# Second norm's modulation on VectorE, the exponentials' table loaded in the output projection, and zero products ahead of routing matmuls

## The chip, the cores and the metric

One core of a Trainium2 chip runs the whole program. The metric is the device time of one execution in microseconds (us). PE is TensorE (matmuls), DVE VectorE, ACT ScalarE, POOL GpSimd, SP SyncE; ACT, POOL and SP also issue DMAs.

## The reference

Two layers of a diffusion backbone over 256 latent tokens and 256 context tokens, each row 1024 wide, all in float32. Each layer first mixes tokens (three attention-like mixers, gated, then an output projection) and then runs a mixture of 16 experts with top-2 routing. What bears on the change, from `hybrid_layer` and `moe_ffn`, cut:

```python
ctx = ctx + mc[2] * mix[:, :L]
x = x + m[2][:, None] * mix[:, L:]
hc = modulate(rms_norm(ctx, norm2), mc[3], mc[4])          # h * (1 + scale) + shift
hx = modulate(rms_norm(x, norm2), m[3][:, None], m[4][:, None])
...
probs = jax.nn.softmax((h @ w_router).astype(jnp.float32), axis=-1)
sel = (probs + b_router.astype(jnp.float32)).reshape(N, N_GROUPS, EXPERTS_PER_GROUP)
...
return (jax.nn.silu(xblk @ w_gate[e]) * (xblk @ w_up[e])) @ w_down[e]
```

Layer 0 does this for context and latent rows (512 rows, four tiles of 128), layer 1 for the latent rows alone (two tiles).

## The kernel before

The program is recorded through a layer that reorders instructions on each engine by their dependences, from the order of the code and from priorities; `issue_after` ties the start of a block to an instruction. All weights come from HBM through SP's queue into a few slots ahead of their use. For float32 precision a weight block is split by ACT into a rounded part `whi` (line 231) and by DVE into the rest `wlo` (line 232), and PE makes three products of each (lines 243 to 245).

The output projection (`output_projection`, lines 900 to 945) splits the merged mixers' output into `mh` and `ml`, then runs through two column halves `dh`; each has two weight pieces and every piece two pairs of `whi` and `wlo`. At the end of a tile and half, `done` adds the gated result to `x` (lines 921 and 922). `vectors` issues small loads from ACT's queue behind the last `mh` cast, in layer 0 also the broadcast rows `m34` (shift and scale of the second norm, line 840) and the norm's weight; a DVE product (line 1080) turns `m34[:, r, 1]` into (1 + scale) times the norm's weight.

`tile_done` (from line 1083) follows each tile of the second half: transposes, sum of squares, `rstd_of`, the router's eight matmuls (line 1099). In layer 0 ACT scales the row, POOL multiplies and adds the modulation in two halves (lines 1104 and 1105), and SP writes the row to `h2d` in HBM. In layer 1 ACT makes `hh` and DVE `hl` (line 1110), for the last tile POOL does so in two operations (lines 1113 and 1114). After each second tile `route` (line 1211) runs a long chain of small DVE operations from `mx` (line 1218) and the exponentials (line 1220) through `se` (line 1225) to `ohb`, the one-hot experts of the pair (line 1257). PE counts ranks from `ohb` (lines 1263 and 1264, the rank matmuls). In layer 0 `place_tiles` then builds one-hot matrices `M` (line 1299) and multiplies (line 1303) to place rows into experts' slots; `indices` makes `gix` (line 1324), by which POOL's indirect DMA gathers the rows of an expert from `h2d` (line 1361). The first expert begins with transposes of `xg` (line 1388). In layer 1 `place_group` gathers by products with `Mg` (line 1342). A branch for overflowing experts stands behind the routing.

`keep_warm` (line 136) multiplies zeros (`idle`, 128x32, against 512 columns) and is called at the program's start only. ACT keeps one table of functions at a time; the exponentials need a load ahead of them (ACT_TABLE_LOAD).

Of the kernel before, what the change touches and what calls it, by code (L numbers as in the profile page):

```python
# [12 lines left out]
F32 = mybir.dt.float32  # L13
# [5 lines left out]
AF = mybir.ActivationFunctionType  # L19
ALU = mybir.AluOpType  # L20
AX = mybir.AxisListType
# [46 lines left out]
def mk(ap, off, dims):  # L68
    return bass.AP(tensor=ap.tensor, offset=ap.offset + off, ap=[list(ap.ap[0])] + [list(d) for d in dims])
# [7 lines left out]
def kernel(es, tc, A, out, dbg=None):  # L77
    nc = tc.nc
    V, S, G, PE, SY = nc.vector, nc.scalar, nc.gpsimd, nc.tensor, nc.sync
# [7 lines left out]
    sm = es.enter_context(tc.tile_pool(name="sm", bufs=2))  # L87
# [3 lines left out]
    RAW_BUFS = 3  # L91
    ARAW = 1
    WARM0, WARM1 = 14, 4
    ORDER = "x0 x1 x2 x3 a0 w0 a1 a2 a3 w1 a4 a5 a6 a7"
    pb = {}

# [23 lines left out]
    rows = cst.tile([128, 512], F32, name="mr")[0:64, 0:128]  # L120
# [9 lines left out]
    nhalf = cst.tile([128, 8], F32, name="nhalf")  # L130
    V.memset(nhalf, -0.5)

    idle = cst.tile([128, 32], BF16, name="idle")
    V.memset(idle, 0.0)

    def keep_warm(n, tag="d"):
        ps = bank(tag)
        for _ in range(n):
            PE.matmul(ps[0:32], idle, mk(idle, 0, [[0, 16], [1, 32]]), start=True, stop=True)

    keep_warm(WARM0, "t")

# [760 lines left out]
    def output_projection(l, op, mg, x, vectors, loaded, tile_done):  # L903

        full = l == 0
        nt = 4 if full else 2
        mh = op.tile([128, 8, 128 * nt], F32R, name="mh")
        m2 = op.tile([128, 2 if full else 1, D], F32, name="m2")
        bcast_rows(m2, l, 2, 3)
        ml = op.tile([128, 8, 128 * nt], F32R, name="ml")  # L910
        for k in range(8):
            m = mg[k // 4][:, k % 4]
            last = S.copy(mh[:, k], m)
            V.tensor_tensor(ml[:, k], m, mh.bitcast(F32)[:, k], ALU.subtract)

        vectors(last)

        def done(t, dh, ps):
            cs = slice(512 * dh, 512 * dh + 512)
            tm = op.tile([128, 512], F32, name="tm", bufs=2)  # L920
            V.tensor_tensor(tm, ps, m2[:, 1 if full and t < 2 else 0, cs], ALU.mult)
            (V if dh else G).tensor_tensor(x[:, t, cs], x[:, t, cs], tm, ALU.add)

        raws = [raw_piece([A["w_out"][l, 512 * h:512 * h + 512, 512 * dh:512 * dh + 512]])
                for dh in range(2) for h in range(2)]
        for dh in range(2):
            w = []
            ps = {}
            for h in range(2):
                w.append(split_raw(*raws[2 * dh + h]))  # L930
                if dh == 1 and h == 1:
                    loaded()
                for t in range(nt) if dh == 0 or h == 1 else ():
                    for hh in (h,) if dh == 0 else (0, 1):
                        if hh == 0:
                            ps[t] = ps_g() if dh or t < 3 else ps_a()
                        for k in range(4):
                            sl = slice(128 * t, 128 * t + 128)
                            mm3(ps[t], mh[:, 4 * hh + k, sl], ml[:, 4 * hh + k, sl],
                                w[hh][0][:, k], w[hh][1][:, k], hh == 0 and k == 0, hh == 1 and k == 3)  # L940
                    if h == 1:

                        with tc.high_priority() if dh and t == nt - 1 else nullcontext():
                            done(t, dh, ps[t])
                            if dh and t:
                                tile_done(t - 1)
                            if dh and t == nt - 1:
                                tile_done(t)
# [33 lines left out]
    h2d = [tc.dram_tile([512, D], F32, name="h2d0")]  # L982
# [3 lines left out]
    def tail(l, mp, mgp, mg, side, other):  # L986


        full = l == 0
        nt = 4 if full else 2  # L990
        cap = 128 if full else 64
# [3 lines left out]
        x = xp.__enter__().tile([128, nt, D], F32, name="x")  # L995
# [9 lines left out]
        with ExitStack() as ms, ExitStack() as ps_:  # L1005
# [26 lines left out]
            with ExitStack() as rs_:  # L1032
# [13 lines left out]
                wrm = rp.tile([128, len(rr), 8, 16], F32, name="wrm")  # L1046
                blg = rp.tile([128, len(rr), 16], F32, name="blg")

                lgs, placed = [None], None

                def vectors(last):
                    with tc.issue_after(last.ins):
# [31 lines left out]
                def tile_done(t):  # L1084
                    r = 1 if full and t < 2 else 0
                    ss = sm.tile([128, 1], F32, name="ss")
                    hT = rp.tile([128, 8, 128], F32, name="h2T", bufs=2)
                    for g in range(2):
                        pt = ps_t((128, 4, 128))
                        for k in range(4):  # L1090
                            PE.transpose(pt[:, k], x[:, t, 128 * (4 * g + k):128 * (4 * g + k + 1)], ident)
                        (V.tensor_copy if g else S.copy)(hT[:, 4 * g:4 * g + 4], pt)
                    xn = xg[(t + 1) % 2] if full else rp.tile([128, D], F32, name="sq", tag="h2T", bufs=2)
                    S.activation(xn, x[:, t], AF.Square, accum_out=ss)
                    rs = rsx[:, t:t + 1]
                    rstd_of(rs, ss, D)
                    lg = bank("g", (128, 16))
                    for k in range(8):
                        PE.matmul(lg, hT[:, k], wrm[:, r, k], start=k == 0, stop=k == 7)
                    if full:  # L1100
                        S.activation(xn, x[:, t], AF.Copy, scale=rs)
                        for g in range(2):
                            cs = slice(512 * g, 512 * g + 512)
                            G.tensor_tensor(xn[:, cs], xn[:, cs], m34[:, r, 1, cs], ALU.mult)
                            G.tensor_tensor(xn[:, cs], xn[:, cs], m34[:, r, 0, cs], ALU.add)
                        SY.dma_start(h2d[l][128 * t:128 * (t + 1)], xn)
                    else:
                        S.activation(hh[:, t], x[:, t], AF.Copy, scale=rs)
                        if t < nt - 1:
                            V.scalar_tensor_tensor(hl_[:, t], x[:, t], rs, hh.bitcast(F32)[:, t],  # L1110
                                                   ALU.mult, ALU.subtract)
                        else:
                            G.tensor_scalar(xn, x[:, t], rs, None, ALU.mult)
                            G.tensor_tensor(hl_[:, t], xn, hh.bitcast(F32)[:, t], ALU.subtract)
                    if t % 2 == 0:
                        lgs[0] = rp.tile([128, 2, 16], F32, name="lg", bufs=2)
                    V.scalar_tensor_tensor(lgs[0][:, t % 2], lg, rs, blg[:, r], ALU.mult, ALU.add)
                    if t % 2 == 0:
                        return
                    later = route(rp, lgs[0], t, nt, br, wts, comb, ohb, rnk, rnb if full else None, rhs, utr, one, cnt)  # L1120
                    if full:
                        nonlocal placed
                        placed = place_tiles(rp, (t - 1, t), cap, iot, rnb, rhs, cc, None if t < nt - 1 else
                                    lambda g: indices(rp, cc, gix, six, g))
                    later()

                with tc.tile_pool(name=f"wo{l}", bufs=1, side=other) as op:
# [80 lines left out]
        slot_queue()  # L1208
        return xp, x, rest

    def route(rp, lg, t1, NT_, br, wts, comb, ohb, rnk, rnb, rhs, utr, one, cnt):

        t0 = t1 - 1
        T = lambda nm, *w: rp.tile([128, 2] + list(w), F32, name=nm, bufs=2)
        pr, se, a1, o1, o2, e = T("pr", 16), T("se", 16), T("a1", 16), T("o1", 16), T("o2", 16), T("e", 16)
        mx, sm_, v, w = T("mx"), T("sme"), T("v"), T("w", 3)
        bc = lambda x, n, k=1: mk(x, 0, [[k, 2], [0, n]])
        V.tensor_reduce(mx, lg, AX.X, ALU.max, negate=True)
        for i in range(2):
            S.activation(pr[:, i], lg[:, i], AF.Exp, bias=mx[:, i:i + 1], accum_out=sm_[:, i:i + 1])  # L1220
        if t1 == NT_ - 1:
# [37 lines left out]
        last = t1 == NT_ - 1  # L1259
# [29 lines left out]

        return weights  # L1290

    def place_tiles(mo, ts, cap, iot, rnb, rhs, cc, then):

        Ms = []
        for g in range(2):
            ps = ps_a((128, 8, 3))
            for i, t in enumerate(ts):
                M = mo.tile([128, cap, 8], BF16, name="M", bufs=2)
                V.tensor_tensor(M, iot[:, :, 8 * g:8 * g + 8], mk(rnb, 16 * t + 8 * g, [[0, cap], [1, 8]]), ALU.is_equal)
                Ms.append(M)  # L1300
            for e in range(8):
                for i, t in enumerate(ts):
                    PE.matmul(ps[:, e], Ms[-len(ts) + i][:, :, e], mk(rhs, 48 * t + 8 * g + e, [[16, 3]]),
                              start=i == 0, stop=i == len(ts) - 1)
            pc = ps.rearrange("p e c -> p c e")
            dst = cc[:, :, 8 * g:8 * g + 8]
            if ts[0] == 0:
                V.tensor_copy(dst, pc)
            else:
                V.tensor_tensor(dst, dst, pc, ALU.add)  # L1310
            if then:
                r = then(g)
        return r if then else None
# [386 lines left out]
```

## Time and profile before

| | |
|---|---|
| median of 3 runs | 1782.86 us (1781.37 to 1783.88) |
| time of the profiled execution | 1782.55 us |
| its span in the trace | 1780.5 us |
| mean granted clock of TensorE | 0.975 |
| busy: PE, DVE, ACT, POOL | 93%, 59%, 46%, 19% of the span |
| HBM | 370.48 MB read, 17.72 MB written |

The span is what the trace covers; the time lies 2.05 us above it. A granted clock of 1.0 is 2.4 GHz and 0.50 is 1.2 GHz. A timeline row has the start in us, the duration in us, engine, line, operation with output and inputs, and behind `[` how long the engine was idle ahead of it and which instruction ended that.

### The profile page before, as it was taken

The page shows a single profiled execution, that of the slowest core. Times are in us where ns is not written, and L with a number is a line of the kernel's source. Part 1 is how long each engine was busy: PE and PEld are TensorE (multiplying, and loading weights), DVE is VectorE, ACT ScalarE, POOL GpSimd, SP SyncE. Part 2 cuts the span into 40 slices and gives each one's busy share as a digit, 9 for nine tenths or more (in the row PEclk, how much of TensorE's full clock was granted, in tenths as well). Part 3 has the DMA queues.
Part 4 walks back from the last instruction along what each step waited for, and adds up shares of the span by engine and source line. Part 5 has one row for each costly group of instructions (what it writes and reads, how often), then busy time and mean ns, then how long its engine had stood idle before and what let it go on. Part 6 is the DMA issues. An engine that isn't in the chain of part 4 may idle for free. (4 is left out here: it accounts for less than half of the span.)

```text
span 1780.5 us, 24184 instructions
## 1 busy us (share of the span) xinstructions
PE 1663.4 (93%) x8912; PEld 1218.9 (68%) x8913; DVE 1047.0 (59%) x1907; ACT 816.7 (46%) x1353; POOL 345.9 (19%) x343
## 2 busy tenths in 40 slices
PE   8999999999999999599999987999999999799997
PEld 4657677887677888477877765878887887433332
DVE  4328473447876345788888888588548865401101
ACT  3313332336676432378877874434456773201100
POOL 0003130222210134301321113133313202100000
PEclk8999999999999999699999997999999999899999
DMA  9895747523212454599999951422435348899996
GB/s 292 285 306 188 253 156 262 175 83 84 59 49 48 105 204 166 185 344 366 367 330 370 356 186 67 125 84 86 142 94 139 89 99 325 301 387 387 387 353 255
DMA packets 263551, 380.01 MB, mean 213 GB/s; under 512 B 33014, under 2 KB 129782, under 8 KB 257920
## 3 DMA queue, kind: packets, MB, share of 16 engines
q1 hardware_dynamic: 251920, 361.19, 60.2%
q10 hardware_dynamic: 7184, 9.42, 1.7%
q0 software_dynamic: 4320, 7.75, 1.3%
q8 instruction: 74, 1.21, 0.3%
q14 instruction: 53, 0.43, 0.1%
HBM read 370.48 MB, written 17.72 MB: 218 GB/s over the span
## 5 line engine op out<-in xcount | busy, mean ns | idle before, releaser
L232 DVE TENSOR_TENSOR wlo<-wraw,whi 128x1024 fp32r<-128x1024 f32 (+2 forms) x368 | 438.7, 1212 | 179.2 <-ACT whi L231 168.4
L231 ACT CAST whi<-wraw 128x1024 fp32r<-128x1024 f32 (+2 forms) x368 | 369.6, 1023 | 174.9 <-PE psg L245 75.8
L243 PE MATMUL psg<-hTh,whi 128*128 128x512 f32 (+1 forms) x576 | 206.2, 360 | 0.0
L244 PE MATMUL psg<-hTl,whi 128*128 128x512 f32 (+1 forms) x576 | 204.9, 356 | 0.0
L245 PE MATMUL psg<-hTh,wlo 128*128 128x512 f32 (+1 forms) x576 | 204.1, 356 | 0.0
L243 PE MATMUL psg<-whi,hTh 128*128 128x512 f32 (+1 forms) x392 | 148.8, 384 | 2.2 <-ACT hTh L373 2.1
L244 PE MATMUL psg<-wlo,hTh 128*128 128x512 f32 (+1 forms) x392 | 148.3, 379 | 0.0
L245 PE MATMUL psg<-whi,hTl 128*128 128x512 f32 (+1 forms) x392 | 147.6, 380 | 0.5 <-DVE hTl L404 0.4
L243 PEld LDWEIGHTS psg<-hTh,whi 128*128 128x128 f32 x576 | 108.9, 189 | 26.2 <-issue 11.0
L245 PEld LDWEIGHTS psg<-hTh,wlo 128*128 128x128 f32 x576 | 108.9, 189 | 18.8 <-issue 6.1
L1464 PE MATMUL psg<-wraw,xT 128*64 128x512 f32 x512 | 120.5, 595 | 1.1 <-ACTq L1139 0.9
L244 PEld LDWEIGHTS psg<-hTl,whi 128*128 128x128 f32 x576 | 109.2, 190 | 16.1 <-issue 4.0
L243 PE MATMUL psg<-whi,xh 128*128 128x512 f32 x256 | 101.7, 397 | 0.7 <-ACT xh L1389 0.7
L244 PE MATMUL psg<-wlo,xh 128*128 128x512 f32 x256 | 99.9, 390 | 0.0
L245 PE MATMUL psg<-whi,xl 128*128 128x512 f32 x256 | 99.6, 390 | 0.0
L243 PEld LDWEIGHTS psg<-whi,hTh 128*128 128x128 f32 x392 | 74.4, 190 | 19.4 <-ACT hTh L373 3.8
L1464 PEld LDWEIGHTS psg<-wraw,xT 128*64 128x64 f32 x512 | 37.2, 137 | 72.7 <-issue 69.1
L245 PEld LDWEIGHTS psg<-whi,hTl 128*128 128x128 f32 x392 | 74.2, 190 | 16.9 <-DVE hTl L404 1.7
L244 PEld LDWEIGHTS psg<-wlo,hTh 128*128 128x128 f32 x392 | 74.5, 190 | 13.2 <-issue 0.5
L1468 ACT ACTIVATE act<-psg 128x256 f32<-128x256 f32 x16 | 6.1, 384 | 150.7 <-PE psg L1464 129.0
L587 ACT ACTIVATE P<-P,smx 128x512 f32<-128x512 f32 (+1 forms) x96 | 62.2, 648 | 22.2 <-DVE smx L586 19.7
L836 POOL TENSOR_TENSOR mg<-mg,gates 128x512 f32<-128x512 f32 (+1 forms) x32 | 38.1, 1199 | 172.2 <-DVE gates L835 126.3
(413 smaller groups left out, 3285.3 us busy)
## 6 DMA issues: line engine op xcount, KB each, us to landing
wraw<-in_w_down_dram SPq DMA_DIRECT2D x64, 1024.0 KB
wraw<-in_w_ada_dram SPq DMA_DIRECT2D x40, 1024.0 KB
wraw<-in_w_in_dram SPq DMA_DIRECT2D x144, 256.0 KB
wraw<-in_w_up_dram SPq DMA_DIRECT2D x32, 1024.0 KB
wraw<-in_w_gate_dram SPq DMA_DIRECT2D x32, 1024.0 KB
wraw<-in_w_gate_dram SPq DMA_DIRECT2D x64, 512.0 KB
wraw<-in_w_up_dram SPq DMA_DIRECT2D x64, 512.0 KB
wraw<-in_w_in_dram SPq DMA_DIRECT2D x24, 1024.0 KB
```

The source lines that it names most:

```text
L231: S.copy(hi[:, :, 0:n], r[:, 2 * j:2 * j + 2, 0:n])
L232: V.tensor_tensor(lo[:, :, 0:n], r[:, 2 * j:2 * j + 2, 0:n], hi.bitcast(F32)[:, :, 0:n], ALU.subtract)
L243: PE.matmul(ps, ah, bh, start=start, stop=False)
L244: PE.matmul(ps, ah, bl, start=False, stop=False)
L245: PE.matmul(ps, al, bh, start=False, stop=stop)
L587: S.activation(flat, flat, AF.Exp, scale=-1.0, bias=m[:, 0:1], accum_out=m[:, 2:3])
L836: G.tensor_tensor(dst, dst, sg[:, i], ALU.add)
L1464: PE.matmul(pgu[64 * c:64 * c + 64, :], xT[:, 2 * p + k, o:o + 64], r[:, :, k, 256 * c:256 * c + 256], start=p == 0 and k == 0, stop=p == ...
L1468: S.activation(a, pgu[:, 0:256], AF.Silu)
```

## The change

Four edits. `tile_done` in layer 0 computes the modulated row by two DVE operations over the whole row of 1024 (a scaled product with `m34[:, r, 1]`, then the addition) instead of ACT's copy and four POOL operations; in layer 1 the last tile's `hl` comes from the same DVE operation as the others'. For the last tile of either layer these stand inside `route`, issued after `mx`. `output_projection` issues a small exponential on ACT behind `vectors`, so the table is loaded there. `keep_warm` runs in three more places: 28 products after the first pair's last placement matmul (layer 0, `WARMR[0]`), 24 after the last router matmul (layer 1, `WARMR[1]`), and 20 after the last placement matmul (layer 0, `WARMG`).

```diff
--- before.py
+++ after.py
@@ -91,6 +91,7 @@
     RAW_BUFS = 3
     ARAW = 1
     WARM0, WARM1 = 14, 4
+    WARMR, WARMG = (28, 24), 20
     ORDER = "x0 x1 x2 x3 a0 w0 a1 a2 a3 w1 a4 a5 a6 a7"
     pb = {}
 
@@ -136,7 +137,8 @@
     def keep_warm(n, tag="d"):
         ps = bank(tag)
         for _ in range(n):
-            PE.matmul(ps[0:32], idle, mk(idle, 0, [[0, 16], [1, 32]]), start=True, stop=True)
+            last = PE.matmul(ps[0:32], idle, mk(idle, 0, [[0, 16], [1, 32]]), start=True, stop=True)
+        return last
 
     keep_warm(WARM0, "t")
 
@@ -915,6 +917,9 @@
 
         vectors(last)
 
+        with tc.issue_after(last.ins):
+            S.activation(sm.tile([128, 8], F32, name="warm"), nhalf, AF.Exp)
+
         def done(t, dh, ps):
             cs = slice(512 * dh, 512 * dh + 512)
             tm = op.tile([128, 512], F32, name="tm", bufs=2)
@@ -1046,7 +1051,7 @@
                 wrm = rp.tile([128, len(rr), 8, 16], F32, name="wrm")
                 blg = rp.tile([128, len(rr), 16], F32, name="blg")
 
-                lgs, placed = [None], None
+                lgs, placed, placed_pe = [None], None, [None]
 
                 def vectors(last):
                     with tc.issue_after(last.ins):
@@ -1096,32 +1101,40 @@
                     rstd_of(rs, ss, D)
                     lg = bank("g", (128, 16))
                     for k in range(8):
-                        PE.matmul(lg, hT[:, k], wrm[:, r, k], start=k == 0, stop=k == 7)
-                    if full:
-                        S.activation(xn, x[:, t], AF.Copy, scale=rs)
-                        for g in range(2):
-                            cs = slice(512 * g, 512 * g + 512)
-                            G.tensor_tensor(xn[:, cs], xn[:, cs], m34[:, r, 1, cs], ALU.mult)
-                            G.tensor_tensor(xn[:, cs], xn[:, cs], m34[:, r, 0, cs], ALU.add)
-                        SY.dma_start(h2d[l][128 * t:128 * (t + 1)], xn)
-                    else:
+                        last = PE.matmul(lg, hT[:, k], wrm[:, r, k], start=k == 0, stop=k == 7)
+                    if not full:
                         S.activation(hh[:, t], x[:, t], AF.Copy, scale=rs)
-                        if t < nt - 1:
+
+                    def rows():
+
+                        if full:
+                            V.scalar_tensor_tensor(xn, x[:, t], rs, m34[:, r, 1], ALU.mult, ALU.mult)
+                            V.tensor_tensor(xn, xn, m34[:, r, 0], ALU.add)
+                            SY.dma_start(h2d[l][128 * t:128 * (t + 1)], xn)
+                        else:
                             V.scalar_tensor_tensor(hl_[:, t], x[:, t], rs, hh.bitcast(F32)[:, t],
                                                    ALU.mult, ALU.subtract)
-                        else:
-                            G.tensor_scalar(xn, x[:, t], rs, None, ALU.mult)
-                            G.tensor_tensor(hl_[:, t], xn, hh.bitcast(F32)[:, t], ALU.subtract)
+
+                    if t < nt - 1:
+                        rows()
                     if t % 2 == 0:
                         lgs[0] = rp.tile([128, 2, 16], F32, name="lg", bufs=2)
                     V.scalar_tensor_tensor(lgs[0][:, t % 2], lg, rs, blg[:, r], ALU.mult, ALU.add)
                     if t % 2 == 0:
                         return
-                    later = route(rp, lgs[0], t, nt, br, wts, comb, ohb, rnk, rnb if full else None, rhs, utr, one, cnt)
+                    if t == nt - 1:
+
+                        with tc.issue_after((placed_pe[0] if full else last).ins):
+                            keep_warm(WARMR[l])
+                    later = route(rp, lgs[0], t, nt, br, wts, comb, ohb, rnk, rnb if full else None, rhs, utr, one, cnt,
+                                  rows if t == nt - 1 else None)
                     if full:
                         nonlocal placed
                         placed = place_tiles(rp, (t - 1, t), cap, iot, rnb, rhs, cc, None if t < nt - 1 else
-                                    lambda g: indices(rp, cc, gix, six, g))
+                                    lambda g: indices(rp, cc, gix, six, g), placed_pe)
+                        if t == nt - 1:
+                            with tc.issue_after(placed_pe[0].ins):
+                                keep_warm(WARMG)
                     later()
 
                 with tc.tile_pool(name=f"wo{l}", bufs=1, side=other) as op:
@@ -1208,14 +1221,17 @@
         slot_queue()
         return xp, x, rest
 
-    def route(rp, lg, t1, NT_, br, wts, comb, ohb, rnk, rnb, rhs, utr, one, cnt):
+    def route(rp, lg, t1, NT_, br, wts, comb, ohb, rnk, rnb, rhs, utr, one, cnt, meanwhile):
 
         t0 = t1 - 1
         T = lambda nm, *w: rp.tile([128, 2] + list(w), F32, name=nm, bufs=2)
         pr, se, a1, o1, o2, e = T("pr", 16), T("se", 16), T("a1", 16), T("o1", 16), T("o2", 16), T("e", 16)
         mx, sm_, v, w = T("mx"), T("sme"), T("v"), T("w", 3)
         bc = lambda x, n, k=1: mk(x, 0, [[k, 2], [0, n]])
-        V.tensor_reduce(mx, lg, AX.X, ALU.max, negate=True)
+        first = V.tensor_reduce(mx, lg, AX.X, ALU.max, negate=True)
+        if meanwhile:
+            with tc.issue_after(first.ins):
+                meanwhile()
         for i in range(2):
             S.activation(pr[:, i], lg[:, i], AF.Exp, bias=mx[:, i:i + 1], accum_out=sm_[:, i:i + 1])
         if t1 == NT_ - 1:
@@ -1289,7 +1305,7 @@
 
         return weights
 
-    def place_tiles(mo, ts, cap, iot, rnb, rhs, cc, then):
+    def place_tiles(mo, ts, cap, iot, rnb, rhs, cc, then, last=[None]):
 
         Ms = []
         for g in range(2):
@@ -1300,8 +1316,8 @@
                 Ms.append(M)
             for e in range(8):
                 for i, t in enumerate(ts):
-                    PE.matmul(ps[:, e], Ms[-len(ts) + i][:, :, e], mk(rhs, 48 * t + 8 * g + e, [[16, 3]]),
-                              start=i == 0, stop=i == len(ts) - 1)
+                    last[0] = PE.matmul(ps[:, e], Ms[-len(ts) + i][:, :, e], mk(rhs, 48 * t + 8 * g + e, [[16, 3]]),
+                                        start=i == 0, stop=i == len(ts) - 1)
             pc = ps.rearrange("p e c -> p c e")
             dst = cc[:, :, 8 * g:8 * g + 8]
             if ts[0] == 0:
```

Where the instructions stand now. DVE in the output projection of layer 0; `m` is `m34`, `xg` the norm's weight. Before:

```order
L232 TENSOR_TENSOR wlo<-wraw,whi 128x1024 [waits DMAHW4_49,Activation_49]
L914 TENSOR_TENSOR ml<-mg,mh 128x512 [waits Activation_49]
L232 TENSOR_TENSOR wlo<-wraw,whi 128x1024 [waits DVE_49,Activation_49]
L232 TENSOR_TENSOR wlo<-wraw,whi 128x1024 [waits DMAHW6_49,DVE_49,Activation_49]
L232 TENSOR_TENSOR wlo<-wraw,whi 128x1024 [waits DVE_49,Activation_49]
L921 TENSOR_TENSOR tm<-psg,m_5499 128x512 [waits PE_49] x2
L1080 SCALAR_TENSOR_TENSOR m_5488<-m_5488,xg_5478 128x1024 [waits DMAHW3_49,DMAHW2_49,DVE_49]
L1080 SCALAR_TENSOR_TENSOR m_5488<-m_5488,xg_5478 128x1024
L921 TENSOR_TENSOR tm<-psg,m_5499 128x512 [waits PE_49,Pool_49]
```

and with the change:

```order
L234 TENSOR_TENSOR wlo<-wraw,whi 128x1024 [waits DMAHW4_49,Activation_49]
L916 TENSOR_TENSOR ml<-mg,mh 128x512 [waits Activation_49]
L1085 SCALAR_TENSOR_TENSOR m_5488<-m_5488,xg_5478 128x1024 [waits DMAHW3_49,DMAHW2_49,DVE_49]
L234 TENSOR_TENSOR wlo<-wraw,whi 128x1024 [waits Activation_49]
L234 TENSOR_TENSOR wlo<-wraw,whi 128x1024 [waits DMAHW6_49,Activation_49]
L234 TENSOR_TENSOR wlo<-wraw,whi 128x1024 [waits Activation_49]
L926 TENSOR_TENSOR tm<-psg,m_5499 128x512 [waits PE_49] x2
L1085 SCALAR_TENSOR_TENSOR m_5488<-m_5488,xg_5478 128x1024
L926 TENSOR_TENSOR tm<-psg,m_5499 128x512 [waits PE_49,Pool_49]
```

The first `m34` product, which waits for two DMA queues, moved from behind three `wlo` subtracts and two `tm` to ahead of the three subtracts.

PE in layer 0's routing, from the last placement matmul of the first pair of tiles (`rhs,M`) to the first rank matmuls of the second pair. Before:

```order
L1303 MATMUL psa<-rhs,M 128x3
L1264 LDWEIGHTS utr
L1264 MATMUL psa<-ohb,utr 128x16 [waits DVE_49]
L1263 LDWEIGHTS one
L1263 MATMUL psa<-ohb,one 128x16
```

and with the change, the last placement matmul, the first and last of 28 such pairs of a load and a zero product, and the rank matmuls:

```order
L1319 MATMUL psa<-rhs,M 128x3
L140 LDWEIGHTS idle
L140 MATMUL psd<-idle 32x512
L1280 LDWEIGHTS utr
L1280 MATMUL psa<-ohb,utr 128x16 [waits DVE_49]
L1279 LDWEIGHTS one
L1279 MATMUL psa<-ohb,one 128x16
```

The zero products are ahead of the rank matmuls in PE's order; they wait for nothing themselves.

DVE in layer 1's routing, from `mx` on. Before:

```order
L1117 SCALAR_TENSOR_TENSOR lg<-psg,rsx,blg 128x16 [waits PE_49,Pool_49]
L1218 TENSOR_REDUCE mx<-lg 128x2 [waits DVE_49]
L1223 RECIPROCAL sme<-sme 128x2 [waits Activation_49]
L1225 SCALAR_TENSOR_TENSOR se<-pr,sme,br 128x16 [waits DMAHW1_49,DVE_49]
L1225 SCALAR_TENSOR_TENSOR se<-pr,sme,br 128x16
L1232 TENSOR_TENSOR m_14229<-se 128x16 [waits DVE_49]
```

and with the change:

```order
L1122 SCALAR_TENSOR_TENSOR lg<-psg,rsx,blg 128x16 [waits PE_49,Pool_49]
L1231 TENSOR_REDUCE mx<-lg 128x2 [waits DVE_49]
L1115 SCALAR_TENSOR_TENSOR hl<-x,rsx,hh 128x1024 [waits Activation_49]
L1239 RECIPROCAL sme<-sme 128x2 [waits Activation_49]
L1241 SCALAR_TENSOR_TENSOR se<-pr,sme,br 128x16 [waits DMAHW1_49,DVE_49]
L1241 SCALAR_TENSOR_TENSOR se<-pr,sme,br 128x16
L1248 TENSOR_TENSOR m_14295<-se 128x16 [waits DVE_49]
```

The product `hl` of 128x1024 now stands between `mx` and the reciprocal of the exponentials' sum.

## Rows read from the trace of the kernel before

**Rows 1.** The page's slices: granted clock of TensorE, 40 slices of 44.5 us.

```profile
PEclk8999999999999999699999997999999999899999
```

**Rows 2.** PE's waits, experts of both layers: us in total, times, longest.

```profile
PE psg L243 <- ACT ah L1410: 10.2, 13, 1.2
...
PE pst L1478 <- DVE act L1469: 1.9, 2, 0.9
```

**Rows 3.** Windows: us, busy by engine (rows), granted clock, DMA share, GB/s.

```profile
11.00:12.00 1.00, 1.00 (x4) 0.27 (x3) 1.00 (x4) 0.97 (x3) 0.00 (x0) 0.64 1.20 299
740.00:750.00 10.00, 2.94 (x39) 2.51 (x38) 7.84 (x43) 0.00 (x0) 1.80 (x2) 0.50 0.39 138
1493.00:1497.00 4.00, 4.00 (x14) 3.15 (x13) 1.08 (x2) 0.00 (x0) 0.76 (x1) 0.57 1.05 386
```

**Rows 4.** Timeline of PE, layer 0: start, duration, row, [idle before it <- releaser].

```profile
741.86 0.17 PE L1264 MATMUL psa<-ohb,utr 128*128 128x16 bf16 x1 [3.06 <-DVE ohb L1257]
...
746.98 1.07 PE L1303 MATMUL psa<-rhs,M 128*128 128x3 bf16 x15 [0.53 <-DVE M L1299]
752.84 1.94 PE L1388 MATMUL pst<-C,xg 128*128 128x128 f32 x8 [4.79 <-DMA xg<-h2d,gix]
```

**Rows 5.** Timeline of DVE, layer 0, routing.

```profile
728.46 1.19 DVE L1244 TENSOR_TENSOR e<-e,C 128x32 f32<-128x32 f32 x1
...
746.84 0.16 DVE L1324 TENSOR_TENSOR gix<-I,J 128x8 uint32<-128x8 f32 x1
```

**Rows 6.** Timeline of PE and of its weight loads at the program's start.

```profile
8.55 5.51 PE L139 MATMUL psd<-idle 128*32 128x512 bf16 x15
...
12.17 0.74 PEld L139 LDWEIGHTS <-idle 128*32 128x32 bf16 x4 [0.34 <-issue]
```

**Rows 7.** Timeline of ACT's queue, DVE and PE, output projection of layer 0.

```profile
668.02 0.45 ACTq L840 DMA_DIRECT2D m<-m_dram  x1
...
669.60 1.23 DVE L232 TENSOR_TENSOR wlo<-wraw,whi 128x1024 fp32r<-128x1024 f32 x1 [1.47 <-ACT whi L231]
...
672.71 0.40 PE L243 MATMUL psg<-whi,mh 128*128 128x512 f32 x1
672.94 0.39 PE L244 MATMUL psg<-wlo,mh 128*128 128x512 f32 x1
```

**Rows 8.** DMA queues from 677 to 678 us: packets, MB, share of 16 engines.

```profile
q10 hardware_dynamic: 8, 0.02, 6.1%
```

**Rows 9.** Line 1110: durations in ns (min/median/max), first and last start.

```profile
L1110 DVE SCALAR_TENSOR_TENSOR hl<-x,rsx,hh x1: 1284/1284/1284, 1506.9 to 1506.9; 128x1024 fp32r<-128x1024 f32 x1
```

**Rows 10.** Timeline of PE, output projection of layer 1.

```profile
1491.58 0.24 PE L1066 MATMUL pst<-C,mrow 24*128 24x24 f32 x1 [1.73 <-DMA mrow<-m_dram]
```

**Rows 11.** Timeline of ACT and DVE, layer 1, routing.

```profile
1515.37 1.28 ACT L1220 ACT_TABLE_LOAD   x1
...
1515.77 0.19 DVE L1218 TENSOR_REDUCE mx<-lg 128x2 f32<-128x32 f32 x1
...
1517.59 2.20 DVE L1225 SCALAR_TENSOR_TENSOR se<-pr,sme,br 128x16 f32<-128x16 f32 x2
```

**Rows 12.** Timeline of PE, layer 1, routing and first group of experts.

```profile
1513.53 1.86 PE L1099 MATMUL psg<-wrm,h2T 128*128 128x16 f32 x8 [0.78 <-DVE rsx L295]
1524.70 0.17 PE L1264 MATMUL psa<-ohb,utr 128*128 128x16 bf16 x1 [9.31 <-DVE ohb L1257]
...
1526.15 0.55 PE L1342 MATMUL psg<-Mg,hh 128*128 128x256 f32 x1 [1.17 <-DVE w L1285]
...
1528.86 0.41 PE L1342 MATMUL psg<-Mg,hh 128*128 128x256 f32 x1
1529.07 0.41 PE L1342 MATMUL psg<-Mg,hl 128*128 128x256 f32 x1
...
1530.96 0.28 PE L1342 MATMUL psg<-Mg,hh 128*128 128x256 f32 x1
1531.08 0.29 PE L1342 MATMUL psg<-Mg,hl 128*128 128x256 f32 x1
```

## The prediction

> **What bounds the kernel now.** I read the 40 slices of the page first: the granted clock of TensorE falls to 0.6 in slice 16 (counted from 0), 0.7 in slice 24 and 0.8 in slice 34 [rows 1]; elsewhere it stays near full speed. Slices 16 and 34 hold the two routing stretches (layer 0: 722 to 755 us, layer 1: 1512 to 1526 us); the change works there. Next, the waits of PE in the two stretches of experts behind them [rows 2]: among the experts no wait is over 1.2 us, in stretches of 345 and 245 us; only the combination that closes the first stretch has a longer one, and it follows the experts. Both stretches are PE's own work, so a routing stretch that ends later or sooner moves the end of the program by the same amount. Third, the routing stretches row by row. In layer 0 PE runs a chain of short pieces and waits between them for DVE, 3.06 us for the second pair's `ohb`, at last 4.79 us for the gather [rows 4], at 0.50 of the clock [rows 3]. DVE is slowed there: a 128x32 product takes 1.19 us while POOL runs the modulation [rows 5], where a reduction of that size takes 0.19 us [rows 11]. In layer 1 the two `se` rows take 2.20 us beside POOL's subtract [rows 11]; PE waits 9.31 us for `ohb` [rows 12].
>
> The profiled execution took 1782.55 us, 0.31 below the median of the runs; the sum is made against it. A measurement of this kernel tells about 0.2% (3.6 us) from no change.
>
> **Part 1: DVE in the output projection of layer 0.** The diff does not name it, but the new order puts the first `m34` product ahead of three `wlo` subtracts; before, it stood behind them and two `tm`. Its data are issued at 668.02 [rows 7] and are still arriving after 677 us: eight packets of that queue, 0.02 MB, lie in the microsecond from there [rows 8]. DVE takes its rows in order, so the `wlo` that began at 669.60 [rows 7] now begins after landing (677.6 to 678.2) plus the product, 1.28 us by the like row [rows 9]: with its own 1.23 us it ends near 680.4. PE's order has 24 matmuls of the second half, from 672.71 on, each 0.233 us behind the other [rows 7], before the first that needs it: it gets there at 678.3. **+2.1 us** (1.2 to 2.8). After an idle of 1.73 us elsewhere in this profile the clock was at a mean of 0.57 for four microseconds [rows 3, 10], which lost 1.7 us; a stall of about the same length may do so here. I take half, **+0.8** (0 to 1.7).
>
> The second table's load moves ahead of a `whi` cast that began at 668.51; the load took 1.28 us [rows 11], and the `wlo` it feeds waits for `m34` longer than that, so it costs nothing; without that wait 24 matmuls, 5.6 us, would still cover it. In layer 1 the same load stands ahead of casts that PE needs only at 1491.6, after a wait for a DMA [rows 10]: nothing.
>
> **Part 2: routing of layer 0.** Off: ACT's scaled copy and four POOL passes per tile. On: two DVE rows of 128x1024 per tile, 1.28 us each by [rows 9]. For the first three tiles DVE has idle time in the dense projection and PE does not wait; for the last they stand behind `mx` in the chain. I laid DVE's new rows one behind another with their durations. Losing the slow rows gives back about 3.4 us, the two new rows cost 2.6, and the second pair's early rows are woven in: the first pair's last placement ends at 739.9 (before 738.8), the second pair's `ohb` at 740.4 (before 741.8). Without fillers gix would come 0.9 us sooner than its 746.84 to 747.0 [rows 5].
>
> But 28 fillers stand between that placement and the rank matmuls of the second pair. The kernel's own opening shows their pace: 15 from 8.55 us on, in 5.51 us [rows 6], with a mean clock of 0.64 in the microsecond from 11 [rows 3]: of the two levels, 1.2 and 2.4 GHz, the lower one until 11.7. So 3.2 us pass cold, 7.5 fillers at 0.427 us (512 columns at 1.2 GHz). Warm, the loads of `idle` follow one another by (0.74 - 0.10)/3 = 0.21 us, with pauses 0.30 on average [rows 6]. So 28 take 3.2 + 20.5 x 0.21 to 0.30 = 7.5 to 9.3 us. I take 8.0: they end at 747.9, the rank matmuls start at 748.0 instead of 741.86 [rows 4], and gix, 4.85 us later, at 752.9: **+5.9 us**. Ends: 3.8 if all run warm (28 x 0.216 = 6.0), 9.7 if all run cold (12.0).
>
> The Trainium skill (PSUM — Partial Sum Buffer, Engine vs sequencer instructions) says that matmuls start and complete in program order. No row here shows a ready matmul held up behind unneeded ones; by the rule the 5.9 stands, without it rank matmuls would start at 740.5, and the term would be -0.9 (the first rival).
>
> Then 20 fillers lie ahead of the first expert's transposes. The gather's transposes began 5.9 us after gix, so now at 758.8. The last placement ends near 753.9; 20 fillers cold at first take 3.2 + 12.5 x 0.21 to 0.30, that is 5.8 to 7.0 us, and the branch among them between nothing and the 4.8 us in which it was hidden [rows 4]; I take 0.5. They end at 760.7, 1.9 too late; a warm PE then saves 1.1 on the eight transposes (1.94 us, [rows 4]) and the first matmuls. **+0.8** (-1.2 to +4.4).
>
> **Part 3: routing of layer 1.** Before: `mx` 1515.77, exponentials behind a table load of 1.28, `se` until 1519.79 [rows 11]. Now without the load: the exponentials and the reciprocal need 0.9 us, from 1516.0 to 1516.9 (before from the load's end, 1516.65, to `se` at 1517.59); the DVE product of 1.28 behind `mx` ends at 1517.2, and the reciprocal and `se`, about 0.2 us a row without POOL, end at 1517.7: **-2.1** (-1.3 to -2.4). `ohb` is then ready at 1522.5. The 24 fillers start behind the router matmuls at 1515.4 [rows 12], and end after 3.2 + 16.5 x 0.21 to 0.30, at 1522.1 to 1523.5: **+0.3** (0 to 1.0). PE then is warm or not when the `Mg` products come: one followed the other by 0.21 us at the low clock, by 0.12 at the high one [rows 12]. The low stretch held about 20 of them: 20 x 0.09 = 1.8. An idle of 1.17 us before them remains [rows 12], and one of 1.73 elsewhere let the clock fall [rows 10], so **-0.8** (0 to -1.9). In the last stretch the order of one pair's transposes moves; the two waits of that kind are 1.9 us in all [rows 2]: **-0.4** (0 to -0.9).
>
> **Sum.** 2.1 + 0.8 + 5.9 + 0.8 - 2.1 + 0.3 - 0.8 - 0.4 = +6.6; 1782.55 + 6.6 = **1789.2 us**. Slower, because the fillers of layer 0 stand ahead of work that is ready.
>
> **The rivals.**
> *The fillers hold nothing up (faster).* If the rank matmuls of the second pair begin within half a microsecond of `ohb`, the 28 fillers cost nothing and the last 20 run warm: 2.1 - 0.9 - 1.2 - 2.1 - 1.9 - 0.4 = -4.4, 1778.1 us. It decides at 2 fillers: more than that do not fit between 739.9 and 740.4. For it: 3.06 us of idle stood at this place [rows 4]. Against it: that idle shrinks to half a microsecond by part 2, since placement and `ohb` come closer. 0.14.
>
> *Cheap fillers, no stall (no difference).* If `m34` lands 2 us sooner than I read, PE finds its weights ready, and if all fillers run warm as well: 0 + 3.8 + 0 - 2.1 - 0.8 - 0.4 = +0.5, 1783.0 us. For it: PE is in dense work until shortly before, and small matmuls may keep the clock up. Against: it was 0.50 through the whole stretch [rows 3]. 0.24.
>
> *The fillers do not raise the clock (much slower).* If the change does not do what it says, 28 take 12.0 us (+9.7), 20 take 8.5 (+4.4), 24 take 10.2 and end 1.0 behind the old start: 2.9 + 9.7 + 4.4 + 1.0 = +18, about 1800.6 us. For it: short stops between the rows. Against: 15 of them raised it in the opening [rows 3, 6]. 0.06. The Trainium skill (TensorE: Matmul & The Clock Gate, Part 1) says that the moment of the rise differs from run to run; no run here shows that. A shift by the 3.2 us of the opening would by it move the end of the 28 by 1.6 us (an estimate).
>
> **How the numbers follow.** My forecast has 0.56. Its own terms reach from 1782 to 1794 us. Slower by over 0.2%: forecast and last rival, 0.62; within 0.2%, 0.24; faster by more, 0.14. The range of 8 in 10 leaves out the faster rival (0.14) and the far end of the last one: 1780.0 to 1794.0 us.
>
> **What would show it.** Right: between 677 and 681 us PE idles about 2 us on DVE's `wlo`; fillers run from 740 to 748 with the rank matmuls directly behind them; the first gather starts near 754 instead of 747.9; in layer 1, counted from `mx`, the first `m` row begins 1.9 us later instead of 4.05. Wrong: rank matmuls that wait for `ohb` in the second pair, a projection without a stall, or experts of layer 0 that start less than 4 us later, against the end of the projection, than before.

## The result and the profile after

| | before | after |
|---|---|---|
| median (4 runs each) | 1782.89 us | 1793.86 us (1789.51 to 1794.34) |
| ratio | | 1.0057, 95% interval 1.0039 to 1.0074 |
| span of the profiled execution (its time) | 1780.5 us (1782.55) | 1787.8 us (1789.51) |

Slower by 10.2 us, 7.0 to 13.2 by the interval. The profiled execution of the change is the fastest of its four: it issues the `m34` load at 664.29 instead of 668.02, 3.7 us earlier, in code that the change doesn't touch. Over all runs below that moment lies between 664.3 and 670.7, so I compare stretch by stretch and use whole times only with their intervals. The stretches below add up to the 7.3 us between the two profiled executions; the slower executions, 4 to 5 us above the profiled one, left no trace.

TensorE's granted clock after, by slices; slice 16 is at 0.7 instead of 0.6, slice 34 at 0.9 instead of 0.8 [rows 1]:

```profile
PEclk9999999999999999799999998999999999999999
```

The clock is higher, and the program slower. In the output projection of layer 0 (timelines of ACT's queue, DVE and PE):

```profile
664.29 0.40 ACTq L842 DMA_DIRECT2D m<-m_dram  x1
...
674.29 1.22 DVE L1085 SCALAR_TENSOR_TENSOR m<-m,xg 128x1024 f32<-128x1024 f32 x1 [10.14 <-DMA m<-m_dram]
675.43 3.49 DVE L234 TENSOR_TENSOR wlo<-wraw,whi 128x1024 fp32r<-128x1024 f32 x3
...
676.70 0.50 PE L246 MATMUL psg<-wlo,mh 128*128 128x512 f32 x1 [2.22 <-DVE wlo L234]
```

DVE stands 10.14 us before the `m34` product, three `wlo` follow as one block, and PE waits 2.22 us. Before, the `wlo` began 1.58 us after the issue of `m34` and PE had no wait there [rows 7]. The idle is followed by a lower clock, 0.62 where the kernel before had 1.00 (windows of before, then of the change: us, busy by engine, granted clock, DMA share, GB/s):

```profile
677.00:681.50 4.50, 4.50 (x21) 3.64 (x20) 3.22 (x4) 0.00 (x0) 2.92 (x2) 1.00 1.03 379
677.00:681.50 4.50, 4.50 (x14) 3.52 (x14) 3.54 (x5) 0.00 (x0) 1.53 (x2) 0.62 0.78 245
```

That is 4.5 x 0.38 = 1.7 us lost behind the idle. A later low clock of the same projection is not the stall's: it stands in before and in the change alike (again before, then the change):

```profile
690.00:700.00 10.00, 10.00 (x43) 8.24 (x44) 1.71 (x4) 2.29 (x3) 0.57 (x1) 0.83 0.21 80
690.00:700.00 10.00, 10.00 (x45) 8.22 (x45) 2.60 (x5) 1.15 (x2) 0.57 (x1) 0.83 0.22 83
```

Layer 0's routing (timelines of PE, then of DVE and POOL):

```profile
739.61 7.70 PE L140 MATMUL psd<-idle 128*32 128x512 bf16 x28
747.24 0.18 PE L1280 MATMUL psa<-ohb,utr 128*128 128x16 bf16 x1
...
753.17 2.74 PE L140 MATMUL psd<-idle 128*32 128x512 bf16 x6
757.08 3.18 PE L140 MATMUL psd<-idle 128*32 128x512 bf16 x14 [1.17 <-PEq L1152]
760.19 1.09 PE L1404 MATMUL pst<-C,xg 128*128 128x128 f32 x8
```

```profile
739.81 0.18 DVE L1273 TENSOR_TENSOR ohb<-o,o 128x32 bf16<-128x32 f32 x1
747.56 0.19 DVE L1281 SCALAR_TENSOR_TENSOR rnk<-psa,ohb 128x32 f32<-128x32 f32 x1 [5.96 <-PE pst L1289]
...
752.47 1.28 POOL L1377 DMA_INDIRECT xg<-h2d,gix  x1 [26.19 <-SPq L1152]
```

`ohb` of the second pair is complete at 739.99. The rank matmuls that need only it start at 747.24, directly behind the 28, and DVE waits 5.96 us for them: where PE waited for DVE before [rows 4], DVE now waits for PE. The gather starts at 752.47 instead of 747.89 (before, POOL):

```profile
747.89 1.28 POOL L1361 DMA_INDIRECT xg<-h2d,gix  x1 [15.86 <-SPq L1139]
```

The transposes behind the last 20 take 1.09 us instead of 1.94 [rows 4].

Layer 1's routing (timelines of DVE, then PE):

```profile
1523.66 0.19 DVE L1231 TENSOR_REDUCE mx<-lg 128x2 f32<-128x32 f32 x1
1523.77 1.28 DVE L1115 SCALAR_TENSOR_TENSOR hl<-x,rsx,hh 128x1024 fp32r<-128x1024 f32 x1
...
1525.15 0.38 DVE L1241 SCALAR_TENSOR_TENSOR se<-pr,sme,br 128x16 f32<-128x16 f32 x2
```

```profile
1523.22 7.56 PE L140 MATMUL psd<-idle 128*32 128x512 bf16 x24
1530.71 0.18 PE L1280 MATMUL psa<-ohb,utr 128*128 128x16 bf16 x1
...
1532.23 0.36 PE L1358 MATMUL psg<-Mg,hh 128*128 128x256 f32 x1 [1.24 <-DVE w L1301]
```

`se` takes 0.38 us instead of 2.20 and begins 1.49 us behind `mx` instead of 1.82 [rows 11]. The `Mg` products start at the high clock, 0.36 us instead of 0.55 for the first [rows 12].

One loss lies in the last stretch, at the branch for overflowing experts of layer 1. Before:

```profile
1702.98 2.37 PE L1464 MATMUL psg<-wraw,xT 128*64 128x512 f32 x10 [0.91 <-ACTq L1139]
```

and after, with the window around it:

```profile
1708.54 4.06 PE L1480 MATMUL psg<-wraw,xT 128*64 128x512 f32 x10 [2.06 <-PEq L1152]
...
1702.00:1712.00 10.00, 7.94 (x30) 2.52 (x28) 0.42 (x1) 0.38 (x1) 0.00 (x0) 0.83 1.05 387
```

The wait grew by 1.15 us, and the clock fell behind it.

Both profiled executions, stretch by stretch (times in us, from rows as above; each stretch runs from one named row's start to the next):

| stretch | before | after | difference |
|---|---|---|---|
| issue of `m34`, from the program's start | 668.02 | 664.29 | -3.7 |
| P: to the last matmul of the projection | 53.79 | 57.83 | +4.0 |
| Q: to the second pair's rank matmuls | 20.05 | 25.12 | +5.1 |
| G: to the first expert's transposes | 10.98 | 12.95 | +2.0 |
| W: to its fourth matmul | 3.18 | 2.27 | -0.9 |
| to the projection's last matmul in layer 1 | 754.11 | 755.54 | +1.4 |
| R: to the rank matmuls of layer 1 | 14.57 | 12.71 | -1.9 |
| M: to the first up matmul | 8.57 | 6.75 | -1.8 |
| E: to the end | 247.21 | 250.29 | +3.1 |

### The profile page after: what moved, and what is told of

Read it like the earlier page. It is cut to its first block, busy times and chain, and to the rows that moved or that the text cites. A ratio compares the mean times of both kernels' runs of the same rounds, so it can differ in the third digit from the quotient of the medians.

```text
span 1787.8 us, 24307 instructions
## 1 busy us (share of the span) xinstructions
PE 1683.3 (94%) x8984; PEld 1225.2 (69%) x8985; DVE 1048.5 (59%) x1916; ACT 811.8 (45%) x1351; POOL 318.6 (18%) x325
## 3 DMA queue, kind: packets, MB, share of 16 engines
q0 software_dynamic: 4320, 7.75, 1.3%
## 5 line engine op out<-in xcount | busy, mean ns | idle before, releaser
L245 PEld LDWEIGHTS psg<-hTh,whi 128*128 128x128 f32 x576 | 108.3, 188 | 26.1 <-issue 10.1
L246 PEld LDWEIGHTS psg<-wlo,hTh 128*128 128x128 f32 x392 | 74.6, 190 | 13.2 <-issue 0.5
```

The lines of the kernel that those rows point to most:

```text
L245: PE.matmul(ps, ah, bh, start=start, stop=False)
L246: PE.matmul(ps, ah, bl, start=False, stop=False)
```

## The experiments

Theory A: the 28 hold up ready work, and DVE's new order stalls the projection; the modulation on DVE and layer 1's fillers gain. Rival B took a different form for each edit, stated with it. Each ratio is against the kernel before on the same chip.

**Fillers of layer 0.** With `WARMR, WARMG` changed, a count of zero leaving the call out:

```diff
-    WARMR, WARMG = (28, 24), 20
+    WARMR, WARMG = (0, 24), 20     # e1
+    WARMR, WARMG = (0, 24), 0      # e3
+    WARMR, WARMG = (28, 24), 0     # e8
```

> The changed kernel without the 28 zero products ahead of the second pair's rank matmuls in layer 0; the other two groups stay. Theory A (fillers hold up ready work): rank matmuls of the second pair start about 740.5 to 741.5 against 747.24 with the 28, on the same clock of the projection's end, and the whole run is 5 to 6 us faster than the change, about 1788 us. Rival B (the 28 pay for themselves by a warm clock behind them; the loss is elsewhere): within 2 us of the change, 1792 to 1796 us.

> The changed kernel without the 28 and without the 20 zero products of layer 0; the 24 of layer 1 stay. Theory A: transposes of the first expert start when its gather has landed, 5.8 us after gix, but cold: they and the first matmuls take 1.1 us more. Against the run without the 28: 0.5 to 2.5 us faster. Rival B (the 20 hide fully in the gather's latency and buy a warm start): 1 us slower than the run without the 28.

> The changed kernel without the 20 zero products ahead of the first expert; the 28 and the 24 stay. Theory A: rank matmuls of the second pair directly behind the 28, 7 us later than without; 6 to 8 us slower than the run without both groups of layer 0, that is 8 to 10 us slower than before. The branch wait in layer 1 (2.0 us in the three runs with the 20, 0.9 in the two without): 0.9 if it goes with the 20, 2.0 if it goes with the 28.

Measured: e1 1.0004 (0.9984 to 1.0025), e3 1.0011 (0.9994 to 1.0028), e8 1.0032 (1.0019 to 1.0044). PE in e1, at the second pair's rank matmuls:

```profile
745.92 0.17 PE L1280 MATMUL psa<-ohb,utr 128*128 128x16 bf16 x1 [0.37 <-DVE ohb L1273]
```

Now they wait 0.37 us for `ohb`. Q is 17.91 us in e1 and 17.22 in e3, 25.18 in e8 and 25.12 in the change: the 28 cost 7 to 8 us. The whole times say the same less sharply: e1 is 9 us below the change, more than the 5 to 6 expected, and e8 only 4 us above e3, less than the 6 to 8 expected, with 2 to 4 us to either side in each interval. For the 20, G is 13.01 us with them (e1) and 11.05 without (e3), W is 2.25 against 3.33: net 0.9 us lost, the lower half of what I expected. Behind the 28 they cost more: G is 12.95 in the change and 10.07 in e8, W 2.27 against 3.32, net 1.8 us. The whole times can tell neither. Behind the 28 alone (e8) W is 3.32, no shorter than before: the granted clock was 0.50 again from 760 to 768 us. Rival B fell for the 28.

**The order of `m34`.** e2 is the change and e4 the change without layer 0's fillers, both with the product tied behind the `wlo` subtracts (`lows` collects these; part of the edit):

```diff
-                        for r in rr:
-                            V.scalar_tensor_tensor(m34[:, r, 1], m34[:, r, 1], 1.0, n2, ALU.add, ALU.mult)
+                        with tc.issue_after(lows[-3].ins):
+                            for r in rr:
+                                V.scalar_tensor_tensor(m34[:, r, 1], m34[:, r, 1], 1.0, n2, ALU.add, ALU.mult)
```

> The changed kernel with the first m34 product tied behind the wlo subtracts, as before; all fillers stay. Theory A (in-order DVE blocks wlo for m34, then the clock falls): the 2.2 us idle of PE in the projection and the low clock behind it (0.83 over 690 to 700 us) are gone, 3 to 4 us faster than the change, about 1790 us. Rival B (the stall is absorbed before the routing's end): within 1 us of the change, 1793 to 1795 us.

> Both repairs: first m34 product behind wlo, no fillers in layer 0; modulation on DVE, the table loads and the 24 fillers of layer 1 stay. Theory A (the change's loss is these two, the rest gains about 3.7 us in layer 1): 1779 to 1782 us, 1 to 4 us faster than before. Rival B (something else lost, in the start or in the last stretch where a branch wait of 2.06 us and a low clock stand in the trace of the change): 1784 to 1788 us.

Measured: e2 1.0053 (1.0031 to 1.0074), e4 0.9978 (0.9960 to 0.9997). e4 against e3 is about 6 us faster and went as theory A said. e2 against the change is not: 1.0053 against 1.0057, a miss, although P fell to 54.05 us, 3.8 less than in the change. In its profile the 28 took 8.98 us and the last 14 5.03, against 7.70 and 3.18 in the change; Q and G together are 2.5 us longer, and M is 9.13 instead of 6.75. The profiled execution (1785.80) lies 6 us below the median of e2's nine, which reach from 1785.75 to 1798.95, so the rest I can't separate from the spread. What e2 was to take away included the low clock from 690 to 700 us; e2 has it too (0.83), as before has. The stall in e1, where the order is the change's (DVE, then PE):

```profile
679.28 1.23 DVE L1085 SCALAR_TENSOR_TENSOR m<-m,xg 128x1024 f32<-128x1024 f32 x1 [12.02 <-DMA m<-m_dram]
...
681.70 0.80 PE L246 MATMUL psg<-wlo,mh 128*128 128x512 f32 x1 [4.10 <-DVE wlo L234]
```

`m34` landed 11.2 us after its issue here, 10.0 in the change's profile; PE's wait is 4.10 us instead of 2.22, and P 59.95. In e3 it landed 11.6 us after issue, the wait is 4.4 us, and P 61.79. My repair is not clean either: in e2, e4, e7, e10 and e12 another wait of 0.9 us stands in P, for `mcol`. P is 54.1 to 55.9 us in three of them and 59 in e7 and e10, where the clock is low in two places, behind the products of `mcol` and again near P's end. The timeline of PE in e10, and both windows:

```profile
688.92 3.45 PE L1081 MATMUL pst<-wr,mcol 128*128 128x16 f32 x26 [0.93 <-DVE mcol L1073]
...
690.00:700.00 10.00, 10.00 (x43) 8.63 (x43) 1.89 (x5) 1.15 (x2) 0.57 (x1) 0.66 0.28 103
718.00:726.00 8.00, 8.00 (x30) 6.80 (x31) 5.67 (x25) 2.95 (x5) 4.13 (x4) 0.57 0.16 66
```

That the wait brought these is not shown: e9 (below) has no wait over 0.3 us in P, and its clock is as low behind the same products:

```profile
687.00:695.00 8.00, 8.00 (x30) 6.85 (x30) 1.16 (x4) 0.00 (x0) 0.00 (x0) 0.57 0.32 121
```

**One edit at a time.** e5 is the kernel before with the small exponential behind `vectors`, e10 the same with the tie of e2, e6 the change without table load and fillers, e7 the change with the tie and without fillers.

```diff
+        with tc.issue_after(last.ins):
+            S.activation(sm.tile([128, 8], F32, name="warm"), nhalf, AF.Exp)
```

> The kernel before with the early table load alone. Its DVE order puts the first m34 product ahead of three wlo subtracts, as in the change. Theory A (the reorder comes with the table load and costs a stall and a low clock): PE idles 2 to 4.4 us in the projection of layer 0, its end comes 4 to 8 us later against the issue of m34, and layer 1's routing gains 1.3 us at most; 3 to 7 us slower than before. Rival B (the load is a pure gain of 1.3 us in layer 1, the stall belongs to the modulation on DVE): 0 to 2 us faster than before.

> The kernel before with the early table load, and the first m34 product tied behind the wlo subtracts as before. Theory A (the loss of the table load alone, 5 us, is the reorder): no idle of 2 us or more in the projection, and the time is that of before or 1 us faster. Rival B (the load itself delays casts that PE needs): 3 us or more slower than before.

> The change without table load and without any zero products: the modulation on DVE alone, with DVE's m34 order as before. Theory A: no stall in the projection, layer 0's second rank matmuls about 2.5 us sooner after the projection, layer 1 gains 0.3 to 1 us; 2 to 4 us faster than before. Rival B (two DVE products on the chain cost what POOL's lock cost): within 1 us of before.

> Modulation on DVE and early table load, m34 product behind wlo, no zero products at all. Theory A: like the run with the 24 of layer 1 kept, but the first group of Mg products cold: 0 to 2 us slower than that run, 2 to 4 us faster than before. Rival B (the 24 cost as much as they give, since they cover the wait for ohb only when they start cold): the same within 1 us.

Measured: e5 1.0028 (1.0012 to 1.0044), e10 1.0008 (0.9993 to 1.0022), e6 0.9982 (0.9970 to 0.9995), e7 0.9990 (0.9976 to 1.0004). DVE and PE in e5:

```profile
675.86 1.23 DVE L1083 SCALAR_TENSOR_TENSOR m<-m,xg 128x1024 f32<-128x1024 f32 x1 [10.41 <-DMA m<-m_dram]
...
678.27 0.50 PE L244 MATMUL psg<-wlo,mh 128*128 128x512 f32 x1 [2.49 <-DVE wlo L232]
```

The table load alone brings DVE's new order, the stall (P 57.97) and a loss of 5 us; with the order repaired (e10) the stall is gone and 1.4 us are left, from -1.2 to 3.9. The two intervals still overlap a little. The modulation alone (e6) keeps the old order, has no such wait in P (52.17), and shortens Q to 16.76 us, 3.3 less than before, and R to 12.76; G, 12.56 us instead of 10.98, gives 1.6 of that back. It is 3.2 us faster. So each edit by itself: modulation a gain, table load a loss by the order it brings, 28 a loss. e7 is 1.8 us faster than before, where 2 to 4 were expected, and its interval includes no change; its profiled execution is the slowest of its twelve, with P at 59.08.

**Fillers of layer 1.** e9 is e6 with the 24, e11 adds 8 ahead of the first expert, e12 is e7 with 44 in layer 1.

```diff
+    WARMR, WARMG = (0, 24), 0     # e9, without the table load
+    WARMR, WARMG = (0, 24), 8     # e11, without the table load
+    WARMR, WARMG = (0, 44), 0     # e12, with table load and tie
```

> Modulation on DVE and the 24 zero products of layer 1; no early table load, no zero products in layer 0. Theory A: as the run with the modulation alone, with PE filled from the router matmuls to ohb in layer 1 (7.5 us idle there, 24 take 7.6 us from a low clock), so the Mg products run warm: 1 to 2 us faster than the modulation alone, 4 to 5 us faster than before, about 1780 us where before is 1785. Rival B (the clock falls again in the wait for Mg, or the 24 end late): the same as the modulation alone.

> The run with modulation and 24, plus 8 zero products (6 ahead of the branch, 2 behind) before the first expert's transposes of layer 0. Theory A: 8 last 3.4 us at the low clock and the branch about 0.9, against 4.0 us from the last placement to the landing of the gather: transposes 0.3 us later, then warm, 1.1 us saved; within 1 us of the run without them, unless the branch wait of layer 1 goes from 0.9 to 2.0 us. Rival B (any zero product in layer 0 costs): 2 us slower.

> Modulation, table load, m34 behind wlo, 44 zero products in layer 1 and none in layer 0. The branch wait of PE in layer 1: 2.0 us if it goes with the length of PE's program (44 pairs as in the run without the 28), 0.9 us if only products in layer 0 bring it. The 44 take 9.8 us warm or 12 us from a low clock, where 7.3 us were idle: rank matmuls of layer 1 start 2.5 to 4.7 us later than with 24, and the run is 2 to 5 us slower than the one with 24 (1780 us).

Measured: e9 0.9973 (0.9956 to 0.9989), e11 0.9975 (0.9960 to 0.9990), e12 0.9995 (0.9978 to 1.0011). PE in e9, then in e4:

```profile
1512.26 7.75 PE L140 MATMUL psd<-idle 128*32 128x512 bf16 x24
...
1521.45 0.36 PE L1355 MATMUL psg<-Mg,hh 128*128 128x256 f32 x1 [1.23 <-DVE w L1298]
```

```profile
1515.16 5.35 PE L140 MATMUL psd<-idle 128*32 128x512 bf16 x24
1522.72 0.17 PE L1283 MATMUL psa<-ohb,utr 128*128 128x16 bf16 x1 [2.20 <-DVE ohb L1276]
...
1524.22 0.55 PE L1361 MATMUL psg<-Mg,hh 128*128 128x256 f32 x1 [1.24 <-DVE w L1304]
```

The same 24 take 7.75 us when the clock is low as they begin, and 5.35 when it is high. In the first case they end with `ohb`, and M is 6.75 us; in the second, 2.20 us of waiting remain, the clock falls, and M is 8.94, as without fillers (7.84 in e6, 9.07 in e7). The other runs bear it out. With the granted clock at 0.50 as they begin (change, e1, e3, e9) the 24 take 7.56 to 8.08 us and M is 6.75 to 6.77; with 1.00 (e2, e4, e11) they take 5.35 and M is 8.76 to 9.13; in e8 the clock rises early among them, they take 6.67, and M is 8.17. So the gain of 1 to 2 us hangs on the clock at their start. In whole times e9 is 1.6 us below e6, and the intervals overlap. e11's 8 let the transposes start 0.18 us behind the gather and warm (W 2.22 us), with no difference in the whole time. In e12 the 44 held the rank matmuls: R 17.21 us against 11.95 in e4, 5.3 us later, a little more than the 2.5 to 4.7 expected. The whole time of e12 is some 3 us above that of e4, as expected, though the two intervals overlap.

**The branch in layer 1.** PE in e12:

```profile
1700.79 4.47 PE L1483 MATMUL psg<-wraw,xT 128*64 128x512 f32 x12 [2.09 <-PEq L1155]
```

The wait is 2.0 to 2.1 us on PE's own sequencer in the change, e1, e2, e8, e11 and e12, and 0.9 to 1.6 us on ACT's queue in before and the other seven. The first group has 32 or more zero products between the program's start-up and that branch, the second 24 or none, and in e12 all stand in layer 1. So it goes with how many of these products PE has, not with where they stand. Why, no run tells. The traces also have the DMA packets that load instructions, 16 KB each: in the first group one starts 3.1 us ahead of the matmul that ends the wait, with 24 products 1.8 us ahead (2.6 in e9), with none 5.9 to 6.0 us ahead and another with the matmul. So the place of these loads moves with the number of products too; whether PE waits for them, no run shows. E is 248.6 to 251.2 us in the first group and 247.2 to 249.1 in the second; in five of the six the clock fell behind the longer wait, and in e2, where it did not, E is 248.58.

## Why the prediction was right, and where it missed

1789.2 us was forecast, with 1780.0 to 1794.0; 1793.86 us came out, at the upper edge. Direction and main mechanism held: the 28 held up ready work, and DVE's order stalled the projection. That the time stayed inside the range is in part luck. In the profile the stretches that the change touches add up to +9.6 us against the +6.6 of the sum: the projection came out 1.1 and the end 3.5 us worse than forecast, layer 0's routing 0.6 and the `Mg` products 1.0 better. The stretch ahead of them, which the change doesn't touch, differs by -3.7, and the long one between the layers by +1.4.

- **The stall in the projection** was forecast as +2.1 us of wait and +0.8 of clock. The change's profile has 2.22 us of wait, 1.7 of clock and +4.0 in P. The landing of `m34`, forecast 9.6 to 10.2 us after issue from one trace, took 10.0. The term that was mis-sized is the clock: I took half of one fall, and a whole one came. This was a mild case: in e1, e3, e5 and e8 the landing takes 10.1 to 11.6 us, the wait is 2.5 to 4.4, and P is 57.8 to 61.8 us, 4 to 8 more than before.
- **The 28 fillers** were forecast to take 8.0 us and hold the rank matmuls by 6.1; they took 7.70, and Q grew by 5.1. A warm filler, 0.21 to 0.30 us in the forecast, took 0.22 (24 in 5.35 us in e4). That they ran from 739.61 to 747.3, so near the 739.9 to 747.9 of the forecast, is partly luck: part 2 left out the 2.9 us that part 1 had added, and the earlier issue of `m34` offset the longer P. Counted from the projection's end they began 0.6 us and ended 0.9 us sooner than forecast. What I had not seen is how much they destroyed. Without them I expected the rank matmuls 1.4 us sooner and gix 0.9; in e3, e4 and e6 Q is shorter than before by 2.8 to 3.3 us, and gix comes 2.7, 3.1 and 1.6 us sooner, counted from the projection's end. My laying out of DVE's rows came out up to 2 us too long.
- **The rule on program order** (the Trainium skill, PSUM — Partial Sum Buffer, Engine vs sequencer instructions) agrees with the trace: `ohb` complete at 739.99, its matmuls at 747.24 behind the last filler. The first rival fell with that.
- **The 20 fillers**: +0.8 forecast, 2.0 - 0.9 = +1.1 in the profile against before, 0.9 and 1.8 in the pairs of runs that differ by them alone.
- **Layer 1**: -2.1 and +0.3 forecast for R, -1.9 found; the first `m` row came 1.91 us behind `mx`, as said. -0.8 for warm `Mg`, -1.8 found: the clock happened to be low as the 24 began; in e4, where it was high, M gained nothing.
- **The last stretch**: -0.4 forecast, +3.1 found. The step that failed is the one that looked only at transposes in another order. It missed the branch, whose wait grew by 1.15 us and was followed by a fall of the clock (0.83 over the ten microseconds shown, 1.7 us).
- **The second rival**, `m34` landing early and warm fillers, was not met in any run with the new order. **The third**, fillers that never raise the clock, fell with 28 in 7.70 us. In the change the granted clock was 0.50 as the 28 began and rose between 742 and 743 us, 3 us into them; in e2 it was 0.50 as well and rose 5.6 us into them. The Trainium skill (TensorE: Matmul & The Clock Gate, Part 1) says that the moment of the rise differs from run to run; these traces agree, with 7.70 and 8.98 us for the same 28.

## What to carry to other kernels

A filler is no idle time filled but work ahead of whatever stands behind it: count how long the engine will wait at that place after the other edits of the same change, since these shortened the wait that the fillers were to cover. After a scheduler has moved instructions, read each engine's order for instructions that wait for a DMA and now stand ahead of others: here an edit on ACT cost DVE 10 us of standing. The parts belong measured one at a time: the modulation with the 24 of layer 1 (e9) is 4.8 us faster than before (0.9973, 0.9956 to 0.9989), faster than the kernel before and the change.

## What the runs showed that I had not expected

The clock moves the time of a stretch as much as the waits do, and not always behind one. 0.93 us of waiting in e10 was followed by a mean clock of 0.66 over 10 us, a wait of the same length in e2 by 0.83, and in e9, with no wait over 0.3 us, the mean was 0.57 over 8 us at the same products. What makes it fall there, no run tells. And with more zero products in PE's program a wait at a branch, up to 950 us behind them, was 2.1 us instead of 0.9.
